# A ring of its own for the modulation loads, sums pinned two units late, and an opening whose order is written out

## The chip, the cores and the metric

The kernel runs on one core of a Trainium2 chip. The metric is the device time of one execution in microseconds (us), a median of several runs. TensorE (PE) multiplies; VectorE (DVE), ScalarE (ACT) and GpSimd (POOL) do the elementwise work; SyncE (SP) issues nearly all loads.

## The reference

Two layers, 256 tokens (two tiles, t = 0 and 1, of 128), width 1024, all in float32:

```python
for layer in range(2):
    shift_m, scale_m, gate_m, shift_f, scale_f, gate_f = split(silu(c) @ ada_w[layer] + ada_b[layer], 6)
    h = rms_norm(x, norm_gains[layer, 0]) * (1 + scale_m) + shift_m
    y = attn_hybrid_mixer(h, w_qkv, w_o, pos) if layer == 0 else retention_mixer(h, w_in, gn_gain, w_o, pos)
    x = x + gate_m * y
    h = rms_norm(x, norm_gains[layer, 1]) * (1 + scale_f) + shift_f
    x = x + gate_f * swiglu(h, w_gate_up[layer], w_down[layer])
return rms_norm(x, final_norm)
```

The attention layer has 8 stick-breaking heads and 8 rotary heads with a softmax; the retention layer has 4 rotary heads. Besides the weights of these products, `ada_w` has to be read: 2 x 1024 x 6144 numbers, of which each row of six vectors per layer is a sum over 1024 rows weighted by silu(c).

## The kernel before

**Products.** Each float32 operand is split into a high and a low part of a format (fp32r) that TensorE multiplies at full rate, and three products stand for one: high x high (L422), low x high (L423), high x low (L426). Weights stream through the kernel in *units* of two 128-row blocks of 512 columns (512 KB). A unit is loaded into a `raw` tile, `wh` is an ACT copy (L220) and `wl` = raw - wh a DVE subtraction (L221), two halves each. A pair (`wh`, `wl`) comes from a pool of `WBUFS` pairs; token tile 0 uses it first, tile 1 trails by 3 units, and by 5 from the attention's output projection on, so the pair is free only after both. `more()` loads and splits one unit ahead of the products.

**Modulation sums.** `ada_unit` loads 128 rows of `ada_w` for one of the six vectors (512 KB, into the same ring of `NRAW` raw tiles) and DVE adds them, weighted, to an accumulator `aacc` (L339, a scalar_tensor_tensor; "sum" below). After eight of them, `ada_mod` folds the accumulators across partitions (L369, an ACT copy L373, L379), or `ada_gate` makes a gate (two halves through ACT L352 and DVE L353, products L357 and L358). `spread` deals these sums over the units.

**The opening.** The first three groups of products (q, k and v of the stick-breaking heads) go over 1024 rows as eight blocks kb. The h of block kb needs the shift and scale of that block alone: `ada0_load` brings columns of `ada_w` (tiles `early`), TensorE sums them (L916), DVE copies the sums (L920), L928 puts them in columns, DVE makes `gm` and `sm` (L931, L933) and h (L942), ACT its high part `hh` (L944), DVE its low part `hl` (L947).

**Order.** TensorE runs in the order of the code. The other engines' orders are chosen by a scheduler with priorities, except where an instruction is pinned (`keep_in_program_order`): it stands behind everything traced before it on its engine. Each engine works strictly in its order. `homes` is the ring of tiles that loads take in turn, and the loads are queued on SP in code order.

Of the kernel before, what the change touches and what calls it, by code (L numbers as in the profile page):

```python
# [15 lines left out]
ALU = mybir.AluOpType  # L16
# [23 lines left out]
GW = 6  # L40
PRIO = 600
WBUFS = 8
NPS = 8
NRAW = 4
WIDE = 2
CONSTS = 4
EARLY = 2
WARM = (5, 1)
# [3 lines left out]
def trunk_kernel(  # L52
# [9 lines left out]
    rawp = ctx.enter_context(tc.tile_pool(name="rawp", bufs=NRAW))  # L62
# [30 lines left out]
    ABLK = ((0, 1, "B1l"), (1, 1, "B0h"), (2, 2, "B0l", "B1h"), (4, 2, None, "B1l"),  # L93
# [229 lines left out]
    def raw_homes(wide):  # L323

        homes[:] = [(rawp, "raw", NRAW)] * NRAW
        if wide:
            homes.extend([(hp, "oqh", 1), (hp, "oql", 1), (wp, "prob", 2), (wp, "sps", 2),
                          (wp, "prob", 2), (wp, "sps", 2)])

    def ada_unit(l, m, kk):  # L330
        if kk == 0:
            a = wp.tile([P, D], F32, tag="aacc", name=nm("aacc"), bufs=2)
            ada_acc[l, m] = a
            nc.gpsimd.memset(a, 0.0)  # L334
            nc.gpsimd.dma_start(a[0:1, :], ada_b[l:l + 1, m * D:(m + 1) * D])
        a = ada_acc[l, m]
        r = raw_tile()
        nc.sync.dma_start(r, ada_w[l, kk * P:(kk + 1) * P, m * D:(m + 1) * D])
        nc.vector.scalar_tensor_tensor(a, r, sc[:, kk:kk + 1], a, op0=ALU.mult, op1=ALU.add)  # L339
# [6 lines left out]
    def ada_gate(l, m):  # L346
        a = ada_acc.pop((l, m))
        g = cp.tile([P, D], F32, tag="gate", name=nm("gate"), bufs=1)
# [14 lines left out]
    def ada_mod(l, m):  # L363
        accs = [ada_acc.pop((l, m)), ada_acc.pop((l, m + 1))]
        yield 4
# [9 lines left out]
        yield 3  # L375
# [19 lines left out]
    def load(i):  # L395
        if i == marks["gu0"] + WIDE or i == marks["gu1"] + WIDE:
            raw_homes(True)
        elif i == marks["ret"]:
            raw_homes(False)
# [510 lines left out]
    def ada0_sum(rs):  # L910
# [8 lines left out]
        rr = w2(None, 2 * w)  # L919
        pin(nc.vector.tensor_copy(rr, p[:, :2 * w]))  # L920
        return rr.rearrange("p (m b f) -> p m b f", m=2, f=P)

    base = {kb: b[0] for b in ABLK for kb in range(b[0], b[0] + b[1])}

    def ada0_mods(kb, rr):
        p2 = pt()
        for m in range(2):
            nc.tensor.matmul(p2[:, m:m + 1], rr[:, m, kb - base[kb]], ones[:, 0:1],  # L928
                             start=True, stop=True)
# [5 lines left out]
    def ada0_block(kb, rr, ts=(0, 1)):  # L935
        k1 = slice(kb, kb + 1)
        if 0 in ts:
            ada0_mods(kb, rr)
# [22 lines left out]
    raw_homes(False)  # L961
    raws = [raw_tile() for g in range(3)]
    for j in range(2):
        for g in range(3):
            nc.sync.dma_start(raws[g][:, j * 512:(j + 1) * 512], units[g * NP][0][:, j, :])
            if g == j == 0:
                nc.sync.dma_start(xt[1], x[0, P:2 * P, :])
        rows.append(ada0_load(1 + j))
    xnT, xns, rstd = [], [], []

    def token_start(t):
        for i in range(2):
            square(t, i)
        rstd.append(rms_rstd(t, nc.vector))
# [5 lines left out]
    def first_split(g, j):  # L980
        c = slice(j * 512, (j + 1) * 512)
        split(ws[g][0][:, c], ws[g][1][:, c], raws[g][:, c])
# [4 lines left out]
    columns()  # L987
    warm_up(WARM[1])
    xn_T(0, 0)
    rr = ada0_sum(rows.pop(0))  # L990
    gain_columns()
    ws = [w_tiles() for g in range(3)]
    first_split(0, 0)
    token_start(1)
    ada0_block(0, rr, (0,))
    first_split(1, 0)
    first_split(2, 0)
    strict[0] = False

    def next_loads(kb):  # L1000
        if kb % 2 == 0 and kb // 2 + 1 < NP:
            wraw.append([load(g * NP + kb // 2 + 1) for g in range(3)])
        if kb in (0, 2):
            rows.append(ada0_load(kb // 2 + 3))
        elif kb + 1 == KD:
            att_alloc()

    wraw = []
    for kb in range(KD):
        kp, j = divmod(kb, 2)  # L1010
        if j == 0 and kb > 0:
            ws = [prep(r) for r in wraw.pop(0)]
# [135 lines left out]
```

## Time and profile before

| | us |
|---|---|
| median of three runs | 771.63 (769.98 to 772.52) |
| the profiled execution | 772.73 |
| its span | 770.9 |
| TensorE busy | 733.2 (95%) |
| VectorE busy | 558.4 (72%) |
| ScalarE busy | 405.0 (53%) |

The span is what the trace covers; 1.8 us of the profiled execution lie outside of it. Matmuls are pipelined, so "busy" is not "at peak"; the steady rate of the 512-column products is one in 0.227 us, and at half clock one in 0.427 us.

### The profile page before, as it was taken

The numbers are of one execution on the slowest core, as the hardware profiler recorded it, in microseconds if no ns is written. First come the engines' busy times: TensorE is split into PE (matmuls) and PEld (weight loads), VectorE is DVE, ScalarE is ACT, GpSimd is POOL, SyncE is SP. The second block draws the span as 40 slices with busy tenths as digits, with TensorE's granted clock in tenths as the row PEclk, the third lists the DMA queues.
The fourth block names the chain that finished last, engine by engine and source line by source line (L and its number), as shares of the span: only waits on it lengthen the run. The fifth ranks groups of instructions, "written<-read, shape, count | busy, mean of one in ns | idle before, by whom it ended". The sixth has DMA issues, their size and how long they took to land.

```text
span 770.9 us, 10529 instructions
## 1 busy us (share of the span) xinstructions
PE 733.2 (95%) x3564; PEld 583.7 (76%) x3564; DVE 558.4 (72%) x960; ACT 405.0 (53%) x836; POOL 57.1 (7%) x137
## 2 busy tenths in 40 slices
PE   5999998889999999998999999989999999999996
PEld 2777775667888788787787878767877888888884
DVE  3667998779999599647867768676588666665553
ACT  5348645875655455535545454454575455555531
POOL 1001000110000100010111211202110000000000
PEclk9999999999999999999999999999999999999998
DMA  9977888667999879627564747666847787655301
GB/s 306 364 254 244 278 286 292 194 229 252 369 353 333 290 268 393 241 82 217 180 216 142 222 145 226 217 211 201 281 146 214 224 238 211 209 182 180 127 1 54
DMA packets 114806, 174.91 MB, mean 227 GB/s; under 512 B 7496, under 2 KB 71184, under 8 KB 114752
## 3 DMA queue, kind: packets, MB, share of 16 engines
q1 hardware_dynamic: 113376, 171.86, 68.7%
q10 hardware_dynamic: 816, 1.60, 0.6%
q0 software_dynamic: 560, 0.77, 0.3%
q8 instruction: 28, 0.46, 0.3%
q14 instruction: 26, 0.21, 0.1%
HBM read 173.16 MB, written 1.05 MB: 226 GB/s over the span
## 4 chain that ended last, share of the span: by engine, by line
PE 71%; DMA 10%; DVE 8%; ACT 4%; issue 3%; POOL 2%; SPq 0%; DVEq 0%; ACTq 0%; POOLq 0%
PE acc L422 22%; PE acc L426 22%; PE acc L423 21%; DMA raw<-in_ada_w_dram 5%; DVE wl L221 3%; DMA raw<-in_att_w_qkv_dram 2%; DMA raw<-in_att_w_o_dram 2%; ACT wh L220 2%; DVE aacc L339 1%; PE pt L795 1%; DMA early<-in_ada_w_dram 1%; DMA raw<-in_ffn_w_gate_up_dram 1%; PE pt L916 1%; POOL v L248 1%; ACT w L286 1%
## 5 line engine op out<-in xcount | busy, mean ns | idle before, releaser
L221 DVE TENSOR_TENSOR wl<-raw,wh 128x512 fp32r<-128x512 f32 x456 | 297.6, 686 | 123.5 <-ACT wh L220 121.1
L220 ACT ACTIVATE wh<-raw 128x512 fp32r<-128x512 f32 x456 | 265.3, 624 | 208.7 <-PE acc L426 101.4
L422 PE MATMUL acc<-wh,hh 128*128 128x512 f32 x640 | 258.7, 404 | 8.6 <-ACT hh L944 6.8
L423 PE MATMUL acc<-wl,hh 128*128 128x512 f32 x640 | 251.0, 392 | 0.0
L426 PE MATMUL acc<-wh,hl 128*128 128x512 f32 x640 | 205.4, 396 | 0.8 <-DVE hl L290 0.8
L422 PEld LDWEIGHTS acc<-wh,hh 128*128 128x128 f32 x640 | 120.9, 189 | 36.6 <-ACT hh L944 7.6
L426 PEld LDWEIGHTS acc<-wh,hl 128*128 128x128 f32 x640 | 119.6, 189 | 27.8 <-DVE hl L290 2.0
L423 PEld LDWEIGHTS acc<-wl,hh 128*128 128x128 f32 x640 | 121.2, 189 | 23.3 <-issue 0.2
L339 DVE SCALAR_TENSOR_TENSOR aacc<-raw,sc,aacc 128x1024 f32<-128x1024 f32 x80 | 102.4, 1279 | 18.4 <-DMA raw<-in_ada_w_dram 17.2
L422 PE MATMUL acc<-wh,act 128*128 128x512 f32 x240 | 94.1, 392 | 0.0
L423 PE MATMUL acc<-wl,act 128*128 128x512 f32 x240 | 93.5, 389 | 0.0
L426 PE MATMUL acc<-wh,act 128*128 128x512 f32 x240 | 74.3, 391 | 0.0
L422 PEld LDWEIGHTS acc<-wh,act 128*128 128x128 f32 x240 | 45.1, 188 | 10.0 <-ACT wh L220 0.8
L423 PEld LDWEIGHTS acc<-wl,act 128*128 128x128 f32 x240 | 45.1, 188 | 9.2
L426 PEld LDWEIGHTS acc<-wh,act 128*128 128x128 f32 x240 | 44.8, 188 | 9.2
L784 ACT ACTIVATE w<-acc 128x256 f32<-128x256 f32 x44 | 16.9, 384 | 28.7 <-PE acc L426 28.7
L785 DVE TENSOR_TENSOR w<-w,acc 128x256 f32<-128x256 f32 x44 | 18.3, 416 | 9.9 <-ACT w L784 9.7
L226 ACT ACTIVATE w<-x 128x512 f32<-128x512 f32 x20 | 12.5, 623 | 19.1 <-DVE x L308 18.3
L334 POOL MEMSET aacc<- 128x1024 f32 x10 | 9.4, 960 | 176.9 <-PE pt L369 86.7
L229 POOL TENSOR_SCALAR ss<-ss 128x1 f32<-128x1 f32 x8 | 2.4, 303 | 266.8 <-ACT w L226 266.8
L740 ACT ACTIVATE w<-w,ry 128x512 f32<-128x512 f32 x8 | 5.8, 724 | 30.3 <-POOL ry L215 30.3
L306 DVE TENSOR_TENSOR w<-acc,gate 128x512 f32<-128x512 f32 x16 | 11.0, 687 | 13.0 <-PE acc L426 13.0
(165 smaller groups left out, 606.3 us busy)
## 6 DMA issues: line engine op xcount, KB each, us to landing
raw<-in_ffn_w_gate_up_dram SPq DMA_DIRECT2D x176, 256.0 KB, 4.5
raw<-in_ada_w_dram SPq DMA_DIRECT2D x80, 512.0 KB, 5.3
raw<-in_ffn_w_down_dram SPq DMA_DIRECT2D x44, 512.0 KB, 4.3
raw<-in_ret_w_in_dram SPq DMA_DIRECT2D x32, 512.0 KB, 4.3
raw<-in_att_w_qkv_dram SPq DMA_DIRECT2D x21, 512.0 KB, 6.2
early<-in_ada_w_dram SPq DMA_DIRECT2D x16, 512.0 KB, 8.6
raw<-in_ret_w_in_dram SPq DMA_DIRECT2D x32, 256.0 KB, 3.9
raw<-in_ret_w_o_dram SPq DMA_DIRECT2D x16, 512.0 KB, 4.7
```

Source lines behind the costliest of these rows:

```text
L220: pin(nc.scalar.activation(hi, src, AF.Copy))
L221: pin(nc.vector.tensor_tensor(lo, src, hi, op=ALU.subtract))
L226: pin(nc.scalar.activation(w2(t), xt[t][:, half * 512:(half + 1) * 512], AF.Square, scale=1.0 / 32.0, accum_out=ss))
L248: pin(g.tensor_scalar(v, s1, s0, None, op0=ALU.add))
L306: nc.vector.tensor_mul(m, ps, gate[:, half * 512:(half + 1) * 512])
L334: nc.gpsimd.memset(a, 0.0)
L339: nc.vector.scalar_tensor_tensor(a, r, sc[:, kk:kk + 1], a, op0=ALU.mult, op1=ALU.add)
L422: nc.tensor.matmul(ps, hi[:, kb, :], a, start=first, stop=False)
L423: nc.tensor.matmul(ps, hi[:, kb, :], b, start=False, stop=False)
L426: nc.tensor.matmul(ps, lo[:, kb, :], wh[:, j * 512:(j + 1) * 512], start=False, stop=last)
L784: nc.scalar.activation(s[:, :256], ps[:, :256], AF.Silu)
L785: nc.vector.tensor_mul(s[:, :256], s[:, :256], ps[:, 256:])
```

## The change

It has three parts. (1) Loads of `ada_w` get three tiles of their own (`NADA`), the others have three instead of four; the sums are pinned on DVE and stand `LATER` = 2 steps behind their loads; loads of units are issued two units ahead (five in the wide stretches of the feed-forward layers); `WBUFS` goes from 8 to 7 to make room; the first six sums of the first gate are loaded within the opening; gates are accumulated in the gate tile itself, and the folding tasks wait longer (`GW`, the numbers in `yield`). (2) The opening is pinned throughout on ACT and DVE: h of the next block and then its splits during the products of the present one. (3) The opening's loads come in halves (256 KB), the second pair of `early` columns as two single blocks, and DVE copies the sums per block.

```diff
-WBUFS = 8
+WBUFS = 7
-NRAW = 4
+NRAW, NADA = 3, 3
+DEPTH = (2, 5)
+LATER = 2
-    ABLK = ((0, 1, "B1l"), (1, 1, "B0h"), (2, 2, "B0l", "B1h"), (4, 2, None, "B1l"),
+    ABLK = ((0, 1, "B1l"), (1, 1, "B0h"), (2, 1, "B0l"), (3, 1, "B1h"), (4, 2, None, "B1l"),
             (6, 2, "B0h", "B0l"))
...
-    def ada_unit(l, m, kk):
+    def ada_load(l, m, kk):
+        if len(due) == NADA:
+            ada_sums(1)
+        r = rawp.tile([P, D], F32, tag="ada", name=nm("raw"), bufs=NADA)
+        nc.sync.dma_start(r, ada_w[l, kk * P:(kk + 1) * P, m * D:(m + 1) * D])
+        due.append((now[0], (l, m, kk, r)))
+    def ada_sums(n):
+        for _ in range(n):
+            ada_unit(*due.pop(0)[1])
+    def step():
+        now[0] += 1
+        ada_sums(sum(at + LATER <= now[0] for at, _ in due))
+    def ada_unit(l, m, kk, r):
         if kk == 0:
-            a = wp.tile([P, D], F32, tag="aacc", name=nm("aacc"), bufs=2)
+            if m in (2, 5):
+                a = cp.tile([P, D], F32, tag="gate", name=nm("gate"), bufs=1)
+            else:
+                a = wp.tile([P, D], F32, tag="aacc", name=nm("aacc"), bufs=2)
...
-        r = raw_tile()
-        nc.sync.dma_start(r, ada_w[l, kk * P:(kk + 1) * P, m * D:(m + 1) * D])
-        nc.vector.scalar_tensor_tensor(a, r, sc[:, kk:kk + 1], a, op0=ALU.mult, op1=ALU.add)
+        tc.keep_in_program_order(nc.vector.scalar_tensor_tensor(
+            a, r, sc[:, kk:kk + 1], a, op0=ALU.mult, op1=ALU.add))
...
     for kb in range(KD):
-        kp, j = divmod(kb, 2)
-        if j == 0 and kb > 0:
-            ws = [prep(r) for r in wraw.pop(0)]
+        late = {0: 0, 1: 2, 2: 1}.get(kb, 0)
+        more_columns = kb + 1 < KD and base[kb + 1] == kb + 1
...
         for g in range(3):
+            if g == late and more_columns:
+                ada0_take()
             if g == 0:
                 next_loads(kb)
+            products(kb, g, (0, 1) if kb else (1,))
+            if g == late and kb + 1 < KD:
+                ada0_mods(kb + 1)
+                ada0_block(kb + 1)
+                w_split(kb + 1)
+            if g == 0:
+                step()
+                for q in {4: (0, 1), 5: (2,), 6: (3, 4), 7: (5,)}.get(kb, ()):
+                    ada_load(0, 2, q)
...
-    spread([(0, 2), (0, 3), (0, 4)], first + 4, marks["gu0"] - 4)
+    spread([(0, 2), (0, 3), (0, 4)], first, marks["gu0"] - 6)
...
-            for e in ada_at.get(i, ()):
-                ada_unit(*e)
-            wts[i] = prep(load(i))
+            load_upto(i + 1 + DEPTH[marks["gu0"] + WIDE <= i < marks["ret"] - DEPTH[1] or
+                                    i >= marks["gu1"] + WIDE])
+            wts[i] = prep(raw_units.pop(i))
+            step()
+            for e in ada_at.get(i, ()):
+                ada_load(*e)
             ready[0] += 1
```

The changed kernel is some lines longer: its L440, L441 and L444 are L422, L423 and L426 of before; L934, L944, L947, L958 and L963 are L916, L920, L928, L942 and L947; L222 is L221, L256 is L255, L357 is the sum L339, L605 is L587, L613 is L595.

Three places show how the orders differ. The first is TensorE at the end of opening block kb = 1 (`acc_252` and `acc_310`, or `acc_248` and `acc_318`, are the third group's accumulators for the two token tiles; `wh_368` and `wh_383` are weights of block 2). Before:

```order
L928 MATMUL pt_349<-mats,w_71_340 128x1 x2
L422 MATMUL acc_252<-wh_193,hh_151 128x512
L423 MATMUL acc_252<-wl_194,hh_151 128x512
L426 MATMUL acc_252<-wh_193,hl_152 128x512
L422 MATMUL acc_310<-wh_193,hh_215 128x512
L423 MATMUL acc_310<-wl_194,hh_215 128x512
L426 MATMUL acc_310<-wh_193,hl_216 128x512
L422 MATMUL acc_244<-wh_368,hh_151 128x512
```

With the change:

```order
L934 MATMUL pt_345<-early_126,sc_94 32x128 x16
L440 MATMUL acc_248<-wh_215,hh_166 128x512
L441 MATMUL acc_248<-wl_216,hh_166 128x512
L444 MATMUL acc_248<-wh_215,hl_167 128x512
L440 MATMUL acc_318<-wh_215,hh_237 128x512
L441 MATMUL acc_318<-wl_216,hh_237 128x512
L444 MATMUL acc_318<-wh_215,hl_238 128x512
L947 MATMUL pt_370<-mats,w_75_368 128x1 x2
L440 MATMUL acc_240<-wh_383,hh_166 128x512
```

The product that makes the columns of block 2 (L928, now L947) stood one group ahead of block 2's first product; now it stands right in front of it, and the sum of its columns (L934) one group ahead.

The second is DVE at the end of the opening. The `wl` named first belong to the units right behind it, `sps` is the low part of a stick-breaking sum that TensorE waits to use (L595, now L613). Before:

```order
L221 TENSOR_TENSOR wl_745<-raw_742,wh_744 128x512
L221 TENSOR_TENSOR wl_760<-raw_757,wh_759 128x512 x2
L221 TENSOR_TENSOR wl_774<-raw_771,wh_773 128x512 x2
L339 SCALAR_TENSOR_TENSOR aacc_797<-raw_800,sc,aacc_797 128x1024
L339 SCALAR_TENSOR_TENSOR aacc_797<-raw_803,sc,aacc_797 128x1024
L339 SCALAR_TENSOR_TENSOR aacc_797<-raw_865,sc,aacc_797 128x1024
L221 TENSOR_TENSOR wl_809<-raw_806,wh_808 128x512
L339 SCALAR_TENSOR_TENSOR aacc_797<-raw_868,sc,aacc_797 128x1024
L587 SCALAR_TENSOR_TENSOR sps_718<-pt_708,w_0_135_720 128x512
L587 SCALAR_TENSOR_TENSOR sps_718<-pt_709,w_0_136_726 128x512
L339 SCALAR_TENSOR_TENSOR aacc_797<-raw_898,sc,aacc_797 128x1024
L221 TENSOR_TENSOR wl_809<-raw_806,wh_808 128x512
```

With the change:

```order
L357 SCALAR_TENSOR_TENSOR gate_687<-raw_569,sc,gate_687 128x1024
L222 TENSOR_TENSOR wl_794<-raw_654,wh_793 128x512
L357 SCALAR_TENSOR_TENSOR gate_687<-raw_640,sc,gate_687 128x1024
L222 TENSOR_TENSOR wl_808<-raw_656,wh_807 128x512
L357 SCALAR_TENSOR_TENSOR gate_687<-raw_692,sc,gate_687 128x1024
L222 TENSOR_TENSOR wl_808<-raw_656,wh_807 128x512
L357 SCALAR_TENSOR_TENSOR gate_687<-raw_694,sc,gate_687 128x1024
L222 TENSOR_TENSOR wl_826<-raw_658,wh_825 128x512
L357 SCALAR_TENSOR_TENSOR gate_687<-raw_722,sc,gate_687 128x1024
L605 SCALAR_TENSOR_TENSOR sps_777<-pt_767,w_0_150_779 128x512
L605 SCALAR_TENSOR_TENSOR sps_777<-pt_768,w_0_151_785 128x512
L222 TENSOR_TENSOR wl_826<-raw_658,wh_825 128x512
```

Before, the halves of four units stood ahead of the first sum, and four sums ahead of `sps`. Now a sum stands ahead of each half, six are ahead of `sps`, and the second half of the third unit (`wl_826`) is behind `sps`, whereas TensorE takes that unit's products before it takes `sps`.

The third is DVE at the start of layer 1, where x of tile 0 is scaled by its norm (L255, now L256), for which TensorE has a transpose waiting (L277). Before:

```order
L221 TENSOR_TENSOR wl_3574<-raw_3570,wh_3573 128x512 x2
L221 TENSOR_TENSOR wl_3588<-raw_3585,wh_3587 128x512
L339 SCALAR_TENSOR_TENSOR aacc_3657<-raw_3660,sc,aacc_3657 128x1024
L255 TENSOR_SCALAR w_0_707_3449<-x_86,ry_3441,ra_3446 128x512
L255 TENSOR_SCALAR w_0_708_3451<-x_86,ry_3441,ra_3446 128x512
L221 TENSOR_TENSOR wl_3588<-raw_3585,wh_3587 128x512
```

With the change:

```order
L222 TENSOR_TENSOR wl_3597<-raw_3451,wh_3596 128x512 x2
L222 TENSOR_TENSOR wl_3611<-raw_3578,wh_3610 128x512 x2
L256 TENSOR_SCALAR w_0_712_3488<-x_86,ry_3480,ra_3485 128x512
L256 TENSOR_SCALAR w_0_713_3490<-x_86,ry_3480,ra_3485 128x512
L222 TENSOR_TENSOR wl_3625<-raw_3594,wh_3624 128x512
```

A sum that stood directly ahead of the two scalings is gone from there.

## Rows read from the trace of the kernel before

**Rows 1.** The page, busy time by engine: us, share of the span, instructions.

```profile
PE 733.2 (95%) x3564; PEld 583.7 (76%) x3564; DVE 558.4 (72%) x960; ACT 405.0 (53%) x836; POOL 57.1 (7%) x137
```

**Rows 2.** Windows: length, busy PE, PEld, DVE, ACT, POOL, granted PEclk, DMA share, GB/s.

```profile
20.00:40.00 20.00, 19.30 (x139) 14.23 (x138) 10.96 (x33) 7.64 (x18) 0.00 (x0) 0.93 1.07 364
98.00:146.00 48.00, 41.73 (x241) 30.02 (x240) 41.75 (x67) 25.54 (x68) 4.20 (x6) 1.00 0.81 267
145.70:149.40 3.70, 3.70 (x19) 3.41 (x18) 3.54 (x9) 2.81 (x8) 0.00 (x0) 0.54 0.52 153
200.00:250.00 50.00, 50.00 (x230) 41.01 (x228) 48.21 (x73) 27.14 (x55) 1.51 (x2) 1.00 1.02 348
507.50:511.00 3.50, 2.97 (x10) 2.58 (x10) 3.50 (x7) 1.23 (x2) 0.00 (x0) 0.51 0.72 252
```

**Rows 3.** PE waits over the span: us in total, times, longest us.

```profile
PE acc L422 <- ACT hh L944: 6.8, 3, 6.1
PE pt L488 <- DVE w L515: 5.5, 3, 3.0
PE pt L277 <- DVE w L255: 4.3, 4, 2.2
PE pt L379 <- ACT w L373: 2.5, 1, 2.5
PE acc L422 <- ACT hh L285: 1.8, 2, 1.4
PE pt L643 <- DVE rc L631: 1.5, 1, 1.5
PE pt L357 <- ACT gh L352: 1.0, 1, 1.0
```

**Rows 4.** Timeline, ACT and DVE, opening: start, duration, engine, line, op, idle before.

```profile
16.27 1.31 ACT L220 ACTIVATE wh<-raw 128x512 fp32r<-128x512 f32 x2 [3.25 <-DMA raw<-in_att_w_qkv_dram]
11.11 0.42 DVE L920 COPY w<-pt 128x256 f32<-128x256 f32 x1 [1.44 <-PE pt L916]
16.93 0.69 DVE L221 TENSOR_TENSOR wl<-raw,wh 128x512 fp32r<-128x512 f32 x1 [2.64 <-ACT wh L220]
```

**Rows 5.** Timeline, PE, opening.

```profile
18.27 0.79 PE L422 MATMUL acc<-wh,hh 128*128 128x512 f32 x1 [6.08 <-ACT hh L944]
27.65 0.50 PE L422 MATMUL acc<-wh,hh 128*128 128x512 f32 x1 [0.30 <-ACT hh L944]
32.70 0.50 PE L928 MATMUL pt<-mats,w 128*128 128x1 f32 x4
34.53 0.39 PE L422 MATMUL acc<-wh,hh 128*128 128x512 f32 x1
62.51 0.39 PE L422 MATMUL acc<-wh,hh 128*128 128x512 f32 x1
```

**Rows 6.** Timeline, PE and DVE, the first stick-breaking sum.

```profile
75.28 1.13 PE L595 MATMUL pt<-sps,amats 128*128 128x512 f32 x2 [0.97 <-DVE sps L587]
74.54 1.28 DVE L587 SCALAR_TENSOR_TENSOR sps<-pt,w 128x512 f32<-128x512 f32 x2
```

**Rows 7.** Timeline, DVE, sums of ada_w ahead of other work.

```profile
113.79 2.60 DVE L339 SCALAR_TENSOR_TENSOR aacc<-raw,sc,aacc 128x1024 f32<-128x1024 f32 x2 [0.16 <-DMA raw<-in_ada_w_dram]
359.42 1.28 DVE L339 SCALAR_TENSOR_TENSOR aacc<-raw,sc,aacc 128x1024 f32<-128x1024 f32 x1 [1.33 <-DMA raw<-in_ada_w_dram]
494.28 1.28 DVE L339 SCALAR_TENSOR_TENSOR aacc<-raw,sc,aacc 128x1024 f32<-128x1024 f32 x1 [1.11 <-DMA raw<-in_ada_w_dram]
```

**Rows 8.** Timeline, ACT, two waits later in the program.

```profile
165.61 1.15 ACT L220 ACTIVATE wh<-raw 128x512 fp32r<-128x512 f32 x2 [2.19 <-DMA raw<-in_ffn_w_gate_up_dram]
501.62 0.73 ACT L740 ACTIVATE w<-w,ry 128x512 f32<-128x512 f32 x1 [5.33 <-POOL ry L215]
```

**Rows 9.** The page, costliest groups: busy us, mean ns | idle before, releaser.

```profile
L220 ACT ACTIVATE wh<-raw 128x512 fp32r<-128x512 f32 x456 | 265.3, 624 | 208.7 <-PE acc L426 101.4
L339 DVE SCALAR_TENSOR_TENSOR aacc<-raw,sc,aacc 128x1024 f32<-128x1024 f32 x80 | 102.4, 1279 | 18.4 <-DMA raw<-in_ada_w_dram 17.2
```


## What I expect, and why

> **What bounds the kernel now.** I read the page first: TensorE is busy 95% of the span [rows 1], so the change can win only what is left, some 38 us, plus time spent at half clock. Next the waits of TensorE [rows 3]: they name who ended each of its gaps. The largest is the 6.1 us ahead of the first product, for the high part of h; then come 1 to 3 us each for a rotated head (L488), the norm of x (L277), the fold of the modulation (L379), the first h of the feed-forward (L285), a softmax (L643) and a gate (L357). DVE or ACT ends them, and the timeline shows why: a sum of 1.28 us [rows 9] stands ahead of the instruction that TensorE needs [rows 7], or ACT is stuck on a copy whose load hasn't landed [rows 4, 8]. The windows then say how full DVE is: 41.75 of 48 us between 98 and 146, 48.21 of 50 between 200 and 250, where TensorE has no gap all the same [rows 2]. So DVE's queue is long, and what matters is its order.
>
> **Opening, first product.** ACT sat 3.25 us on weight copies whose load came late, DVE 2.64 us behind it, and h stood behind both; the product came at 18.27 [rows 4, 5]. Pinned, h goes first. DVE had the column sums at 11.1 [rows 4]. The split of the first group now goes ahead of their copy (0.69), the copy takes 0.42, the product L928 0.5 [rows 4, 5], two tiny DVE steps about 0.4 (an estimate: they are single columns), then h and its copy 0.65 together (18.27 less the end of the split, 17.62): 11.1 + 0.7 + 0.4 + 0.5 + 0.4 + 0.65 = 13.8. I take 14.4, with 0.6 for hops between engines: 3.9 us ahead of before.
>
> **Opening, first to third block.** The norm of token tile 1 ran before the first product; now it follows the splits: two squares of x, scale, transposes, h and its copy, ten or so ACT and DVE steps of 0.3 to 0.7 in a row, 6.5 us. The second tile's products begin near 20.9; block 1 needs 3 more for its own columns, h and split, so starts near 23.9 (before 27.65 [rows 5]), and the lead still stands at 3.8. Block 1 is 18 products of 0.227 plus a column sum of 1.1, until 29.1 or 29.3. Here the first piece of order shows a loss: the columns of block 2 are made right in front of block 2. Before, from L928 to the product was at most 34.53 - 32.70 = 1.8 us [rows 5], with a group of products in between; now nothing covers it, and the weight copy (0.62 [rows 9]) is pinned behind h, so 2.4 us. Block 2 starts near 31.7 instead of 34.53. It holds a column sum that block 1 held before (1.1), and some of L928 again shows (0.5): from block 3 on the lead is about **1.3**. Block 7 starts at 61.2 instead of 62.51 [rows 5].
>
> **First units behind it.** In the second piece of order (with its first sum and half split, which stand just ahead of the rows shown) six sums and five half splits stand between the splits of block 7 and `sps`, and one more half behind it is needed first. Block 7's splits come after h of block 7, behind the first group of block 6, and end near 62.4: block 6 begins a block (4.6) earlier than 61.2, one group takes 1.4, chain and three splits 4.4. Then 6 x 1.27 + 5 x 0.62 + 1.28 + 0.65 = 12.6: 75.0. TensorE ran out of products at 75.28 - 0.97 = 74.3 before [rows 6]; 1.3 earlier, and the half in question begins 0.8 ahead of the end: 72.2. The stall is 2.8 instead of 0.97: **+1.8**. Opening and stall together: +0.5.
>
> **What disappears later**, each with its bounds:
> - Head at 116: two sums (2.60) stood ahead of the rotation [rows 7]; now one sum and a half split. The gap lies between nothing and 2.5 (5.5 in three gaps, the longest 3.0 [rows 3]): **-1.2** (0 to -2.5).
> - Softmax at 127 (1.5 [rows 3]): one of two sums ahead goes: **-0.7** (0 to -1.5).
> - Fold at 141 (2.5 [rows 3]): the task waits longer, so L379 moves behind the softmax. But what follows is that softmax itself, which has its own chain on ACT and DVE, so I leave 1 us of a gap. Behind the old gap the clock stood at 0.54 for 3.7 us [rows 2], that is 1.7 us lost; a smaller gap should spare it. **-2.7** (0 to -4.2).
> - Feed-forward at 166 (1.4 [rows 3]): ACT sat 2.19 us on a load [rows 8]; loads now go two units ahead: **-0.9** (0 to -1.4).
> - Norm at 359 (2.2 [rows 3]): the sum waited 1.33 us for its load and took 1.28 [rows 7]; the third piece of order shows it gone. The norm's scale itself comes late too: **-1.4** (0 to -2.2).
> - Head at 505 (3.0 [rows 3]): the sum at 494.28 (1.11 of wait, 1.28 [rows 7]) goes from ahead of a group norm; its scale is what ACT waited 5.33 us for [rows 8], and the copies behind it fed the sum and rotation that TensorE waited for. One of two sums stays. The clock was 0.51 for 3.5 us behind it [rows 2]. **-2.0** (0 to -4.2).
> - Gate at 526 (1.0 [rows 3]): more time for its task: **-0.9** (0 to -1.0).
>
> **New waits.** ACT's splits waited 101.4 us in all for TensorE to free a weight pair [rows 9]: they run as far ahead as the pairs reach. One pair less lets a split begin one unit later, 12 x 0.227 = 2.7 us, in the stretches where tile 1 trails by five. No wait of a product for `wl` is among the rows, so today there is slack. Three raw tiles instead of four shared ones add to it, and so do a gate's memset and bias on POOL, which now wait for the last reader of the gate before and have the norm's steps queued behind them on POOL. **+1.5**; 0 if all is covered, +5 if some ten such places cost 0.5 each.
>
> **Smaller loads.** Between 20 and 40 the queue already mixed 256 KB and 512 KB and kept the engines full, 364 GB/s at a DMA share of 1.07 [rows 2]; the opening's 15.7 MB (sixteen `early` pieces, twelve units, x) at that rate are 43 us, well before block 7 at 61. I cost the halving at nothing; the bound is the rival on loads below.
> The Trainium skill, "DMA: Bandwidth & Descriptors", section Bandwidth, has a rule to batch transfers to 1 MiB or more for three quarters of the peak; by it the halved loads would lose rate. The trace bears it out little: the 364 GB/s were reached with pieces of a half and a quarter of that.
>
> **Sum.** +0.5 - 1.2 - 0.7 - 2.7 - 0.9 - 1.4 - 2.0 - 0.9 + 1.5 = -7.8. The profiled execution took 772.73, so 764.9; the median before is 1.1 lower than that execution, within the runs' spread of 0.33%, and I take a part of it: **764.5**.
>
> **Rivals.**
> - *The gains are given back* (0.15). DVE is nearly full before 146 and still has 24 sums there; what TensorE gains at one place it waits for at the next. If the terms from 116 to 166 come to nothing and those at 359, 505 and 526 count by half, it is +0.5 - 2.2 + 1.5 = -0.2: 772, no change. For it: those 41.75 of 48 us. Against: the 6.25 us left over.
> - *The lead is kept* (0.16). If the splits are through before `sps`, because DVE does the sums in its gaps between blocks, the stall of 2.8 falls to under 1 (-1.5 instead of +0.5), nothing new waits, and the later terms are full for the most part (-12): 772.7 - 13.5 = 759, or 757 with the median's 1.1.
> - *The pinned sums hold DVE up* (0.20), the slower side. A pinned sum that waits for its load holds all of DVE; before, 17.2 us of such waits [rows 9] mostly cost TensorE nothing. With a sum in front of each half split, a stall like that at `sps` returns at each of the next units until DVE has caught up. At 1.28 for each of six units it is +7.7, and half of the later terms is lost (+5): 764.5 + 12.7, about 777. It decides from some 7 us of added stalls on.
> - *Loads bound the opening* (0.05). At the 267 GB/s of the stretch from 98 to 146 [rows 2], 15.7 MB take 59 us; block 7 then waits and the opening is 1 to 3 us longer, and the sums' loads behind it are late: 768. This is what that rule of the Trainium skill would mean here.
>
> **How the numbers follow.** A measurement here tells about 0.3%, 2.3 us, from no change. The forecast has 0.44, spread over 760 to 769. Faster takes in it, the kept lead and the load case (0.65, and 0.01 of the given-back case); no change takes the rest of the given-back case, 0.14; slower the pinned sums, 0.20. For 8 in 10 the range reaches from 757, the kept lead, to 775, most of the way to the slow case.
>
> **What would show it.** The first product near 14.4, block 2 near 31.7 behind a gap of about 2 us, block 7 at 61.2; a stall of 2 to 3 us between the products of the third unit behind the opening; no wait for the fold near 141 and full clock there; no gap over 1 us ahead of the norm near 355 and the head near 500. I am wrong in the favourable sense if that stall is under 1 us, and in the other if products show waits for `wl` in several places or the sums' waits for their loads grow over 17 us.

## The result, and the profile after

The changed kernel took 768.17 us (median of 7 runs, 766.36 to 770.17), the kernel before, run beside it, 772.52 (7 runs, 769.98 to 773.81): a ratio of 0.9945, with a 95% interval of 0.9926 to 0.9965. It is faster by about 4 us, half of what I forecast. The profiled execution took 768.65, its span is 766.9, against 772.73 and 770.9 before.

The page, busy time by engine (us, share of the span, instructions), to be read against [rows 1]:

```profile
PE 735.1 (96%) x3600; PEld 582.5 (76%) x3600; DVE 558.5 (73%) x963; ACT 403.1 (53%) x836; POOL 56.3 (7%) x137
```

No engine runs fewer instructions than before [rows 1], so the difference lies in waits and in the clock. The waits of TensorE in the changed kernel (us in total, times, longest):

```profile
PE acc L441 <- DVE wl L222: 5.8, 6, 2.8
PE pt L278 <- DVE w L256: 2.5, 4, 0.9
PE acc L440 <- ACT wh L221: 2.3, 2, 1.9
PE pt L661 <- DVE rc L649: 2.2, 2, 1.2
PE pt L506 <- DVE w L533: 1.8, 4, 0.7
PE acc L440 <- ACT hh L960: 1.8, 2, 1.4
```

Beside [rows 3], the largest gap (6.1 us ahead of the first product) is down to 1.4, the rotated head from 5.5 to 1.8, the norm from 4.3 to 2.5, and the waits for a fold and for a gate are off the list. New at its head are products that wait for `wl`, 5.8 us, of which 4.9 lie in two gaps. The timeline of TensorE shows where (start, duration, engine, line, op; in brackets the idle time before and what ended it):

```profile
14.23 0.50 PE L440 MATMUL acc<-wh,hh 128*128 128x512 f32 x1 [1.41 <-ACT hh L960]
17.77 2.19 PE L91 MATMUL pt<-w 128*128 128x512 f32 x4
19.81 0.60 PE L969 MATMUL pt<-mats,w 128*128 128x128 f32 x4
...
25.01 0.49 PE L440 MATMUL acc<-wh,hh 128*128 128x512 f32 x1 [0.39 <-ACT wh L221]
...
30.95 0.50 PE L947 MATMUL pt<-mats,w 128*128 128x1 f32 x4
33.33 0.49 PE L440 MATMUL acc<-wh,hh 128*128 128x512 f32 x1 [1.87 <-ACT wh L221]
...
76.13 0.56 PE L441 MATMUL acc<-wl,hh 128*128 128x512 f32 x1 [2.05 <-DVE wl L222]
79.91 0.80 PE L441 MATMUL acc<-wl,hh 128*128 128x512 f32 x1 [2.81 <-DVE wl L222]
```

The first product comes at 14.23 (before 18.27 [rows 5]), but block 2 only at 33.33, 1.2 us ahead of before, and block 7 at 63.42, 0.9 behind. The two long gaps stand at the third unit behind the opening. The timeline of DVE there:

```profile
62.57 1.90 DVE L222 TENSOR_TENSOR wl<-raw,wh 128x512 fp32r<-128x512 f32 x3 [0.23 <-ACT wh L221]
64.38 1.28 DVE L357 SCALAR_TENSOR_TENSOR gate<-raw,sc,gate 128x1024 f32<-128x1024 f32 x1
...
69.78 1.28 DVE L357 SCALAR_TENSOR_TENSOR gate<-raw,sc,gate 128x1024 f32<-128x1024 f32 x1
...
74.18 1.28 DVE L357 SCALAR_TENSOR_TENSOR gate<-raw,sc,gate 128x1024 f32<-128x1024 f32 x1 [2.53 <-DMA raw<-in_ada_w_dram]
75.39 0.68 DVE L222 TENSOR_TENSOR wl<-raw,wh 128x512 fp32r<-128x512 f32 x1
76.78 1.28 DVE L357 SCALAR_TENSOR_TENSOR gate<-raw,sc,gate 128x1024 f32<-128x1024 f32 x1 [0.71 <-DMA raw<-in_ada_w_dram]
77.98 1.28 DVE L605 SCALAR_TENSOR_TENSOR sps<-pt,w 128x512 f32<-128x512 f32 x2
79.18 0.68 DVE L222 TENSOR_TENSOR wl<-raw,wh 128x512 fp32r<-128x512 f32 x1
```

TensorE goes on at 76.13 and 79.91, right behind the halves that begin at 75.39 and 79.18. Each stood behind a pinned sum whose data came late, the second behind `sps` as well. Why the data was late, the queue of SP shows, and the windows behind it (columns as in [rows 2]):

```profile
52.49 11.17 SPq L424 DMA_DIRECT2D raw<-in_att_w_qkv_dram  x3
65.69 2.14 SPq L335 DMA_DIRECT2D raw<-in_ada_w_dram  x2
```

```profile
58.80:63.30 4.50, 4.50 (x23) 3.55 (x22) 3.42 (x11) 1.88 (x6) 1.76 (x2) 1.00 0.00 0
76.00:84.00 8.00, 5.07 (x10) 2.61 (x10) 7.29 (x10) 1.71 (x4) 0.00 (x0) 0.57 0.83 263
98.00:146.00 48.00, 45.09 (x264) 33.12 (x265) 43.21 (x69) 27.54 (x67) 0.69 (x1) 1.00 0.88 300
```

The first row of SP holds three loads of weights: the third stood 9.7 us at the head of the queue, until the splits of block 7 freed a raw tile and it was issued at 63.29; between 58.8 and 63.3 the DMA engines moved nothing (share 0.00). The loads of `ada_w` behind it could not have gone sooner either, for their ring was full: its three loads were issued by 48.8, but the first sum, pinned behind those splits, ran only at 64.38 and freed its tile near 65.66. The second row of SP holds the next two loads of `ada_w`, issued at 65.69 and 67.49. The sum at 69.78 found the first landed; the sum at 74.18 waited for the second. The mean clock from 76 to 84 was 0.57, so most of that stretch ran at 1.2 GHz. Later the stretch from 98 to 146 is 3.4 us busier than before [rows 2].

### The profile page after: what moved, and what is told of

Same layout as the page of the kernel before. It is cut to its first block, busy times and chain, and to the rows that moved or that the text cites. A ratio compares the mean times of both kernels' runs of the same rounds, so it can differ in the third digit from the quotient of the medians.

```text
span 766.9 us, 10605 instructions
## 1 busy us (share of the span) xinstructions
PE 735.1 (96%) x3600; PEld 582.5 (76%) x3600; DVE 558.5 (73%) x963; ACT 403.1 (53%) x836; POOL 56.3 (7%) x137
## 4 chain that ended last, share of the span: by engine, by line
PE 61%; DVE 7%; ACT 3%; POOL 2%; issue 2%; DMA 2%; DVEq 0%; SPq 0%; ACTq 0%; POOLq 0%
PE acc L444 19%; PE acc L440 19%; PE acc L441 19%; DVE wl L222 3%; ACT wh L221 1%; PE pt L813 1%; DMA raw<-in_ret_w_o_dram 1%; POOL ra L211 1%; DMA raw<-in_ret_w_in_dram 1%; DVE gate L357 1%; ACT w L287 1%; DMA raw<-in_ffn_w_gate_up_dram 0%; DVE w L528 0%; DVE w L256 0%; ACT w L227 0%
## 5 line engine op out<-in xcount | busy, mean ns | idle before, releaser
L222 DVE TENSOR_TENSOR wl<-raw,wh 128x512 fp32r<-128x512 f32 x456 | 297.9, 687 | 135.1 <-ACT wh L221 132.7
L221 ACT ACTIVATE wh<-raw 128x512 fp32r<-128x512 f32 x456 | 265.9, 624 | 207.0 <-PE acc L444 109.7
L440 PE MATMUL acc<-wh,hh 128*128 128x512 f32 x640 | 258.3, 404 | 4.4 <-ACT wh L221 2.3
L441 PE MATMUL acc<-wl,hh 128*128 128x512 f32 x640 | 251.5, 393 | 5.6 <-DVE wl L222 5.6
L444 PE MATMUL acc<-wh,hl 128*128 128x512 f32 x640 | 205.4, 396 | 1.4 <-DVE hl L291 1.4
L440 PEld LDWEIGHTS acc<-wh,hh 128*128 128x128 f32 x640 | 120.4, 188 | 32.5 <-ACT wh L221 3.0
L441 PEld LDWEIGHTS acc<-wl,hh 128*128 128x128 f32 x640 | 120.8, 189 | 31.4 <-DVE wl L222 8.4
L444 PEld LDWEIGHTS acc<-wh,hl 128*128 128x128 f32 x640 | 119.5, 189 | 28.2 <-DVE hl L291 2.9
L440 PE MATMUL acc<-wh,act 128*128 128x512 f32 x240 | 94.4, 393 | 0.0
L441 PE MATMUL acc<-wl,act 128*128 128x512 f32 x240 | 93.7, 390 | 0.2 <-DVE wl L222 0.2
L444 PE MATMUL acc<-wh,act 128*128 128x512 f32 x240 | 74.2, 390 | 0.0
L357 DVE SCALAR_TENSOR_TENSOR aacc<-raw,sc,aacc 128x1024 f32<-128x1024 f32 x48 | 61.4, 1279 | 0.0
L440 PEld LDWEIGHTS acc<-wh,act 128*128 128x128 f32 x240 | 45.1, 188 | 10.4 <-issue 0.8
L441 PEld LDWEIGHTS acc<-wl,act 128*128 128x128 f32 x240 | 45.1, 188 | 9.9 <-DVE wl L222 0.8
L444 PEld LDWEIGHTS acc<-wh,act 128*128 128x128 f32 x240 | 44.9, 188 | 9.4
L357 DVE SCALAR_TENSOR_TENSOR gate<-raw,sc,gate 128x1024 f32<-128x1024 f32 x32 | 40.9, 1278 | 3.2 <-DMA raw<-in_ada_w_dram 3.2
```

The lines of the kernel that those rows point to most:

```text
L221: pin(nc.scalar.activation(hi, src, AF.Copy))
L222: pin(nc.vector.tensor_tensor(lo, src, hi, op=ALU.subtract))
L357: tc.keep_in_program_order(nc.vector.scalar_tensor_tensor(a, r, sc[:, kk:kk + 1], a, op0=ALU.mult, op1=ALU.add))
L440: nc.tensor.matmul(ps, hi[:, kb, :], a, start=first, stop=False)
L441: nc.tensor.matmul(ps, hi[:, kb, :], b, start=False, stop=False)
L444: nc.tensor.matmul(ps, lo[:, kb, :], wh[:, j * 512:(j + 1) * 512], start=False, stop=last)
```

## Experiments

Times are medians, ratios are to the kernel before in the same set of runs, whose medians were 769.89 (E1 to E4), 770.50 (E5 to E8), 771.23 (E9, E10) and 771.97 (E11, E12). "At a unit" compares the start of the same product in two profiled executions, the variant's and that of before. These are single executions: at the end of the program such differences lie between 1 us below (E9) and 4 us above (E1, E5, E7) what the ratio of the medians gives, so they tell where time is won or lost, and the ratios tell how much.

**E1 and E2: the two halves of the change.** The first is the kernel before with the written opening and its smaller loads (no sums in it); the second has the ring, late sums, deeper loads, seven pairs and longer tasks, and the opening of before.

```diff
 E1
-WARM = (5, 1)
+WARM = (5, 1, 2)
-    ABLK = (... (2, 2, "B0l", "B1h"), ...
+    ABLK = (... (2, 1, "B0l"), (3, 1, "B1h"), ...
...
+                ada0_block(kb + 1)
+                w_split(kb + 1)
 E2
-WBUFS = 8
-NRAW = 4
+WBUFS = 7
+NRAW, NADA = 3, 3
+DEPTH = (2, 5)
+LATER = 2
...
+            step()
+                ada_load(*e)
```

> The kernel before with the pinned opening alone: order, half loads, single blocks, sums copied per block; the modulation sums, the rings, eight weight pairs and the loads of the main loop stay as before. Theory A (the opening as pinned gains nothing): the first product comes 4 us earlier, but the lead is gone by block 4 and block 6 starts 0.5 to 1 us later than before; the time is that of before within 0.3% (770 to 774). Rival B (the opening's lead of 4 us is real and lost only at the stall of the first units behind it): block 6 starts 1 us or more earlier and the time is 768 to 770.

> The changed kernel with the opening of before: ring of three for the modulation loads, sums pinned two units late, seven weight pairs, loads ahead, later tasks; the first gate's sums all start behind the opening. Theory A (all of the gain comes from the sums' order in the main loop, and the stall of 4.9 us near 75 from the six sums that the opening loads): the stall near 75 is under 2.5 us, no half clock there, and the time is 763 to 766. Rival B (the pinned sums ahead of the half splits cost the stall wherever they start): 4 us or more of stall between 70 and 85 here too, time 768 or more.

E1: 775.72, ratio 1.0093 (1.0063 to 1.0123), slower by 0.9%. E2: 760.73, ratio 0.9884 (0.9845 to 0.9923), faster than the whole change. By these ratios the opening alone costs some 7 us of 770 and the ring alone gains some 9. For the opening theory A was still too kind, and rival B fell; for the ring theory A was right, and the gain is larger than it gave. In E2 the first unit behind the opening lies 0.8 us ahead, unit 32 (the first feed-forward) 3.5, and the end 11.0. Its waits of TensorE, from the largest:

```profile
PE acc L441 <- ACT hh L963: 6.0, 3, 5.3
PE pt L279 <- DVE w L257: 2.5, 4, 0.9
PE pt L662 <- DVE rc L650: 2.2, 1, 2.2
```

The late first product is back, yet no product waits for `wl`, and the clock from 70 to 85 is 1.00: the stall belongs to the opening with its sums.

**E3 and E4: the sums of the opening.** E3 is the changed kernel without the six early loads (they go to the units behind, where `spread` now deals 24 sums instead of 18); E4 leaves the sums to the scheduler.

```diff
 E3
-                for q in {4: (0, 1), 5: (2,), 6: (3, 4), 7: (5,)}.get(kb, ()):
+                for q in ():
-        seq = [(l, m, q) for l, m in lm for q in range(6 if (l, m) == (0, 2) else 0, KD)]
+        seq = [(l, m, q) for l, m in lm for q in range(KD)]
 E4
-        tc.keep_in_program_order(nc.vector.scalar_tensor_tensor(
-            a, r, sc[:, kk:kk + 1], a, op0=ALU.mult, op1=ALU.add))
+        nc.vector.scalar_tensor_tensor(a, r, sc[:, kk:kk + 1], a, op0=ALU.mult, op1=ALU.add)
```

> The changed kernel without the six modulation loads in the opening; all 24 sums of the attention layer are spread over the units behind it. Theory A (the six sums ahead of the first splits cause the stall of 4.9 us and the half clock behind it): the stall near 75 is under 1.5 us and the products of unit 14 are 4 to 6 us ahead of the changed kernel's; if the lead is kept the time is 763 to 765. Rival B (DVE is full from 62 to 146, so what is won near 75 is paid back by 140 with six more sums there): the products near 142 are no earlier than in the changed kernel and the time is 767 to 769.

> The changed kernel with the sums left to the scheduler (the pin on the weighted sum is taken away; ring, lateness, loads and the opening stay). Theory A (the pin as such matters little; a sum two units behind its load has its data): the scheduler again puts a sum ahead of the first splits, the stall near 75 stays between 2 and 6 us, the later gains (fold at 141, norm at 359, head at 505, gate at 526) stay, time 766 to 770. Rival B (the pin is what keeps sums away from the norm at 359 and the head at 505): the waits there come back with 2 to 3 us each and the time is 770 to 773.

E3: 767.41, ratio 0.9972 (0.9948 to 0.9996). Nothing is lost between 70 and 85 any more (+2.7 at unit 14, +2.3 at unit 17, where the changed kernel goes from +0.9 to +7.4), but the stall returns further on. DVE and TensorE of E3:

```profile
125.24 1.28 DVE L357 SCALAR_TENSOR_TENSOR aacc<-raw,sc,aacc 128x1024 f32<-128x1024 f32 x1 [1.46 <-DMA raw<-in_ada_w_dram]
```

```profile
128.44 0.51 PE L441 MATMUL acc<-wl,oh 128*128 128x512 f32 x1 [2.80 <-DVE wl L222]
```

Again a pinned sum waits for its load, and a product for the half behind it; 3.2 us are lost here and unit 32 stands at +3.6. Rival B, paid back, was right. E4: 763.74, ratio 0.9930 (0.9906 to 0.9954), below what either theory gave. TensorE is busy without a break from 73 to 85 there; 2.6 us are lost earlier instead, as the scheduler puts two sums ahead of h of block 7. The gap at 505 does not come back and that at 359 stays at 0.9, though nothing pins the sums. So the stall of 6 us needs the pin, and the pin isn't what cleared the later places.

**E5: the opening mended.** No warm-up products behind the first block, and the columns of block 2 made a block's length earlier; all else as changed.

```diff
-WARM = (5, 1, 2)
+WARM = (5, 1, 0)
-        late = {0: 0, 1: 2, 2: 1}.get(kb, 0)
+        late = {0: 0, 1: 0, 2: 1}.get(kb, 0)
```

> The changed kernel with two edits to its opening: the two warm-up products ahead of the second tile's transposes are left out (they compute nothing that is used), and the columns of block 2 are made after the first group of block 1 instead of after the third. Theory A (these two places lose the opening's lead): the second tile's first product comes 1.5 us earlier, the gap of 1.9 us ahead of block 2 shrinks under 0.5, block 2 starts 4 us or more ahead of the kernel before, and block 6 at least 1.5 us ahead of the changed kernel's. If the stall near 75 comes from the early sums alone, it grows by as much and the total stays at the changed kernel's within 0.3%. Rival B (loads bound blocks 2 to 4): block 4 starts where it did and new waits for weight copies show between 30 and 45.

762.56, ratio 0.9904 (0.9876 to 0.9932), where theory A had the time of the changed kernel. Its places in the opening came out, save that the second tile's first product is only 0.6 us earlier (1.5 expected). Block 2 starts 4.6 us ahead of before (changed kernel: 1.2), the first unit behind the opening 2.8 ahead (0.9 behind): two numbers of the opening were worth 3.7 us. Then 5.5 us are lost between the first and the third unit, for another reason. TensorE, ACT and a window of this kernel:

```profile
72.23 0.79 PE L440 MATMUL acc<-wh,hh 128*128 128x512 f32 x1 [2.37 <-ACT wh L221]
```

```profile
68.02 1.08 ACT L602 ACTIVATE w<-pt 128x512 f32<-128x512 f32 x2
68.98 1.16 ACT L603 ACTIVATE w<-w 128x512 f32<-128x512 f32 x2
70.02 1.16 ACT L604 ACTIVATE w<-w 128x512 f32<-128x512 f32 x2
71.06 0.60 ACT L871 ACTIVATE att_v<-acc 128x512 f32<-128x512 f32 x1
71.54 2.72 ACT L221 ACTIVATE wh<-raw 128x512 fp32r<-128x512 f32 x5
```

```profile
69.00:80.00 11.00, 8.44 (x20) 5.36 (x21) 10.90 (x14) 7.28 (x15) 0.00 (x0) 0.69 0.86 268
```

The copies of the next weights start at 71.54, behind attention work that fills ACT from 68 to 71, and from 69 to 80 the mean granted clock is 0.69. TensorE got there sooner than the weights. After that this kernel stands at +3.2 where the changed one stands at +7.4, and most of what it gains in the end is this difference.

**E6, E7 and E10: which part of the ring gains.** E6 is E2 with the task delays of before. E7 is the kernel before with seven pairs, nothing else. E10 is E7 with the longer delays.

```diff
 E6
-GW = 12
+GW = 6
...
-        yield 6
+        yield 4
...
-        yield 6
+        yield 3
 E7
-WBUFS = 8
+WBUFS = 7
 E10, beside E7's line
-GW = 6
+GW = 12
...
-        yield 4
+        yield 6
...
-        yield 3
+        yield 6
```

> The kernel with the ring alone (opening of before) and with the folding tasks as short as before (waits of 4 and 3 and 6 instead of 6, 6 and 12). Theory A (the tasks' longer waits are what removes the gaps at the fold near 141 and the gate near 526): both gaps are back, 2.5 us and 1 us, with the half clock behind the first, and the time is 3 to 5 us above the ring alone, 764 to 766. Rival B (earlier loads and pinned sums free DVE and ACT there anyway): the gaps stay under 1 us and the time is within 1.5 us of the ring alone.

> The kernel before with seven weight pairs instead of eight and nothing else. Theory A (the slack of some 6 us between a split's end and its use covers one unit less, 2.7 us): the lead falls to about 4 us in the stretches where tile 1 trails by five, products show under 1 us of waits for wl in all, and the time is that of before within 0.3%. Rival B (the lost pair costs half a microsecond at ten places): 3 to 5 us slower.

> The kernel before with seven weight pairs and the folding tasks' longer waits (12, 6 and 6), without ring, pins, earlier loads or any edit to the opening. Theory A (the pair and the waits are what pays, the ring and its pinned, late sums add nothing): 760 to 763, the ring alone (760.7) within 0.3%, no gap over 1.3 us at the gate near 526. Rival B (the ring adds its own gain, two fewer gaps at 116 and 127): 764 to 766, only the 1 us at the gate better than seven pairs alone (765.1).

E6: 766.53, ratio 0.9950 (0.9930 to 0.9969); its waits of TensorE have in second place, with two waits for gates:

```profile
PE pt L376 <- ACT gh L371: 4.8, 2, 2.9
```

By the ratios the longer delays are worth some 5 us of the ring's 9, most of it at the gates; the fold waits only 0.7, so it doesn't depend on them as I had thought (theory A had 2.5 there). E7: 765.08, ratio 0.9936 (0.9908 to 0.9963), which **neither theory allowed**: I had both at no change or slower. One pair fewer is 5 us faster. DVE ahead of the norm in layer 1, and TensorE's waits that answer to [rows 3], both of E7:

```profile
351.95 1.29 DVE L221 TENSOR_TENSOR wl<-raw,wh 128x512 fp32r<-128x512 f32 x2
353.60 1.40 DVE L221 TENSOR_TENSOR wl<-raw,wh 128x512 fp32r<-128x512 f32 x2 [0.36 <-ACT wh L220]
355.53 1.00 DVE L255 TENSOR_SCALAR w<-x,ry,ra 128x512 f32<-128x512 f32 x2 [0.53 <-POOL ra L251]
```

```profile
PE pt L277 <- DVE w L255: 3.0, 4, 0.9
PE pt L488 <- DVE w L515: 2.0, 3, 1.2
```

The sum of [rows 7] is gone from ahead of the norm, as in the changed kernel, without a ring and without a pin; the gap at 141 is gone and that at 505 down to 0.3. E10: 767.90, ratio 0.9964 (0.9940 to 0.9989), slower than both theories had it and no faster than E7. With longer tasks on top the gate's gap at 526 goes, but ACT, in the shared ring of four tiles, is stuck behind sums:

```profile
124.65 0.63 ACT L220 ACTIVATE wh<-raw 128x512 fp32r<-128x512 f32 x1 [6.74 <-DMA raw<-in_att_w_o_dram]
```

In E2, with the ring of its own, the longest such wait is 4.3 and no product waits for its copy; E10 stands at +2.7 at unit 32 and E2 at -3.5. So the ring carries a share of its own, and it lies ahead of the feed-forward. (E2 also issues its loads further ahead; which of the two brings the share wasn't tried one by one. The pin doesn't: E8 below does without it.) The longer delays pay only with the ring, so the shares don't simply add up.

**E12: a shorter lead in another way.** The kernel before with three raw tiles.

```diff
-NRAW = 4
+NRAW = 3
```

> The kernel before with three shared raw tiles instead of four and nothing else. Theory A (a shorter run-ahead of splits and sums, by whatever buffer, keeps the scheduler from setting a sum ahead of the norm at 359, the group norm at 494 and the fold at 141, as seven pairs did): at least two of these three gaps go, and the time is 764 to 768. Rival B (the raw tiles only delay loads, sums and weights, and the sum stays where it was): the gaps at 359 and 505 stay above 2 us each, and the time is 771 to 777.

788.40, ratio 1.0214 (1.0179 to 1.0249). The gaps at 359 (to 0.95) and 505 (gone) vanish here too, as the theory had it, but the time is far off it, since loads come late in the stretch before 155, where it loses 14 us:

```profile
PE acc L422 <- ACT wh L220: 6.3, 4, 2.5
PE pt L595 <- DVE sps L587: 3.9, 2, 2.4
PE acc L423 <- DVE wl L221: 3.5, 5, 1.8
```

**E8, E9 and E11: better versions.** E8 is E2 with the sums left to the scheduler (the edit of E4). E9 is the mended opening of E5 without early sums (E3) and without the pin (E4). E11 is E9 with the splits of the first three units pinned ahead of the products of block 7, and the ring turned by one for the third pair of opening weights so that the loads of these units find a tile.

```diff
 E11, beside E9
+            if kb == 3:
+                homes.append(homes.pop(0))
             pair_load((kb + 3) // 2)
...
+            if kb + 1 == KD and g == 0:
+                more(first + 3)
             products(kb, g, (0, 1) if kb else (1,))
```

> The ring alone (opening of before) with the sums left to the scheduler. Theory A (what pays is the ring and the earlier loads; the pin itself is neutral): 759 to 763, as the ring alone. Rival B (the pin keeps sums away from the norm at 359 and the head at 505): the gaps there come back and the time is 764 to 767.

> The changed kernel with the mended opening (no warm-up products ahead of the second tile, block 2's columns after the first group), no sums loaded in the opening, and the sums left to the scheduler. Theory A (what the mended opening wins can be kept once no pinned sum stands ahead of the first splits): 2.8 us ahead at unit 12 and no more than 1 us of it lost by unit 17; the time is 755 to 758, under the ring alone unpinned (759.0). Rival B (ACT and DVE carry the first units' splits late however the opening ends, so the lead is lost between units 12 and 17 and by the softmax at 127): the products from unit 32 on stand where those of the ring alone unpinned do, 4 us ahead of before, and the time is 758 to 761.

> The kernel with the mended opening, no sums loaded in it and the sums left to the scheduler (758.5), with one more edit: the splits of the first three units behind the opening are pinned in it, behind those of block 7 and ahead of the attention's copies, and the third pair of blocks takes idle tiles so that the three loads needn't wait. Theory A (the lead of the mended opening is lost between units 12 and 15 because ACT copies the third unit's weights only behind the attention's copies and a table load): no product of units 12 to 14 waits for a weight, unit 15 stands 2.5 to 3 us ahead of before instead of 0.6 behind, and the time is 755 to 757.5. Rival B (what is won there is paid back by the softmax at 127 and the fold, where DVE is full): unit 32 stands 2.5 us ahead of before as without the edit, time 757.5 to 760.

E8: 758.97, ratio 0.9860 (0.9833 to 0.9886), at the lower end of theory A. E9: 758.48, ratio 0.9824 (0.9779 to 0.9869), rival B's 758 to 761: its 2.9 us of lead at the first unit turn into a loss of 0.6 by the fourth, with ACT's copies at 71.52 behind attention work just as in E5. E11: 757.26, ratio 0.9828 (0.9798 to 0.9857), at the upper end of theory A's range (755 to 757.5), but not by its route: the fourth unit stands 0.8 us ahead of before, not 2.5 to 3, and most of what this execution has over E9's is won later, with unit 32 at 7.0 ahead against 2.5. Its waits of TensorE from the largest:

```profile
PE pt L278 <- DVE w L256: 2.5, 4, 0.9
PE pt L505 <- ACT w L514: 1.8, 1, 1.8
```

The stall at the third unit is gone (0.45 us of a gap is left, for `sps`), against one new gap of 1.8 at 64, where the pinned copies hold ACT ahead of a head's rotation. Its median is the lowest of all and it beats both kernels, but it can't be told from E9, whose ratio is 0.9824. The medians put what the mended opening adds to E8 at some 2 us; the intervals overlap, so this isn't shown.

## Why the forecast was right in direction and off in size

Measured here is how much longer or shorter the way between the same two products became from the profiled execution of before to that of after. The fold's own products run in other places than before (L379 at 143.72, as L397 now at 154.96), so its stretch is cut where both kernels have done the same work.

| term of the sum | forecast | measured |
|---|---|---|
| opening, to the first unit behind it | -1.3 | +0.9 |
| stall at the third unit and `sps` | +1.8 | +6.0 |
| head at 116 (measured from 78 to 125) | -1.2 | -3.4 |
| softmax at 127 (to 133) | -0.7 | +1.7 |
| fold at 141 (133 to 156) | -2.7 | -2.6 |
| feed-forward at 166 | -0.9 | -1.1 |
| norm at 359 | -1.4 | -1.3 |
| head at 505 | -2.0 | -4.0 |
| gate at 526 | -0.9 | -0.6 |
| new waits elsewhere | +1.5 | +0.4 |
| sum | -7.8 | -4.0 |

**The step that failed: opening and stall, forecast at +0.5 together, measured at +6.9.**

*Opening.* The first product (14.4 forecast, 14.23) and the 2.4 us from L947 to block 2 (30.95 to 33.33) were right. I left out the two warm-up products (four instructions at L91): they run for 2.19 us right ahead of tile 1's transposes, so block 1 begins at 25.01, not 23.9, and it has 0.6 of gaps for weights in it. E5 shows that they and the place of block 2's columns together cost 3.4 us at block 2. The +0.9 itself is of one execution: with the same order in the opening, block 6 starts 0.8 us behind before in the changed kernel, 1.6 in E1 and 2.3 in E3. The gap there is ACT's order, too: its timeline has

```profile
32.19 0.57 ACT L960 ACTIVATE hh<-w 128x128 fp32r<-128x128 f32 x2 [6.19 <-DVE w L958]
32.66 1.65 ACT L221 ACTIVATE wh<-raw 128x512 fp32r<-128x512 f32 x3
```

so ACT stood 6.19 us at the pinned copy of h, with the weights' copies pinned behind it.

*Stall.* I added up durations on DVE as if the data of the sums had been there, so their waits for it stood in the sum at nothing. The ring has three tiles, and it was full until the first sum, which is pinned behind block 7's splits; so loads came late, DVE waited 2.53 and 0.71 for them, and TensorE had 4.9 us of gaps where it had 0.97 before; the rest of the 6.0, some 2 us, is the half clock from the first of them on. That is the mechanism of the rival "the pinned sums hold DVE up", at one place instead of six; it stayed below the 7 us from which that rival decides. E2, E3 and E4 each take one ingredient away (opening, early loads, pin), and in each the stall at this place is gone; where the pin stays, E3 shows it again at 128. My test for it, waits of sums for loads growing over 17 us, was a poor one: in all they fell from 17.2 [rows 9] to 3.2, and yet the two that are left stand ahead of the 4.9 us of gaps.

**The later terms** from 78 on were -8.3 forecast and -10.9 measured. Fold, feed-forward, norm and gate are right to within 0.3. The heads were sized at half of their bound, and nearly the whole gap went, at 505 with the half clock behind it: 2.6 of gap (3.0 to 0.4) and about 1.5 of clock make the 4.0. Of the 3.4 up to 125, 2.4 are the head at 116; the rest is mostly a wait for `sps` at 97 of 0.8 (its row, L593, I hadn't counted) that is gone. The softmax was wrong in sign. TensorE of the changed kernel has there, and at the feed-forward:

```profile
132.01 0.63 PE L661 MATMUL pt<-mats,w 128*128 128x128 f32 x4 [0.97 <-DVE rc L649]
133.28 0.63 PE L661 MATMUL pt<-mats,w 128*128 128x128 f32 x4 [0.64 <-DVE w L650]
...
137.41 1.09 PE L551 MATMUL pt<-prob,att_v 128*64 128x128 f32 x14 [1.29 <-ACT prob L664]
...
169.06 0.50 PE L440 MATMUL acc<-wh,hh 128*128 128x512 f32 x1 [0.36 <-ACT hh L286]
```

The softmax still waits for its own chain on DVE and ACT, which I had named for the fold alone: 2.9 us of gaps where one of 1.5 was [rows 3]. At the feed-forward the gap of 1.4 [rows 3] is down to 0.36, as forecast.

**New waits** had the wrong sign as far as the pairs go. E7 shows that one pair fewer gains 5 us alone, with the sum gone from ahead of the norm; that this is because splits then run less far ahead is argued. So I put the terms at 359 and 505 down to the ring and the pin, where E7 and E12 show that a shorter lead alone clears them, and E4 that the pin isn't needed. In the changed kernel both causes are there at once, and which did it can't be told apart. That the time still fell as forecast is in part luck: what I counted as a cost, the missing pair, gains by itself as much as the whole change.

**The rivals.** Loads didn't bound the opening: between 14 and 64 no ACT copy of the changed kernel waited for one (before, 4.3 us did). The rule of the Trainium skill on batching to 1 MiB ("DMA: Bandwidth & Descriptors", section Bandwidth) would have had the halves lose rate; from 20 to 40 the queue moved 351 GB/s, before 364 [rows 2], so a little less, and no copy waited for it. I had misread that row of before: its loads of 256 KB had all landed by 17.6, so the 364 were reached with pieces of 512 KB; the smaller ones are tested by the 351 alone, where the loads of weights issued in that stretch are of 256 KB. The lead was not kept: it was gone by block 3.

**Open:** why the scheduler's order tips with the number of pairs just where it does (the runs show that it does, not by which comparison), and why E2 and E5 gain 1.3 to 1.5 us between 366 and 495 where the changed kernel gains nothing with the same code. That ACT could have copied block 2's weights ahead of h was argued from its idle time, and not tried.

## What to carry to other kernels

Before a consumer is pinned, ask what must happen before its data can even be requested: in a ring, the load n tiles later waits for this instruction, so a pin behind a late instruction delays transfers far behind it, and adding up busy times won't show it. Cost each half of a large change by itself: here a loss of 7 us hid in a gain of 9. And how far a scheduler may run ahead (pairs, tiles) is an order knob of its own; try one less before building machinery for the order.

## What the runs showed of the hardware that I had not expected

One waiting load holds SP's whole queue: 9.7 us, of which the DMA engines were idle for 4.5 (58.8 to 63.3). Here it cost nothing by itself, since the loads behind it had no free tile before 65.66. And the length of a gap alone did not tell whether the clock fell. Behind the gap of 2.05 that ended at 76.13 the granted clock was 0.50 (77.1 to 79.9), before the second gap was over, and behind E5's single gap of 2.37 it was 0.50 too (72.2 to 76). In the kernel before, a gap of 2.24 that ended at 361.31 left it at 1.00 (361 to 366), and in E1 one of 2.76 that ended at 512.45 did as well (508 to 516).
